# GpSimd without two-input elementwise work in a scheduled hybrid decoder layer

## The chip, the cores and the metric

The kernel runs on one core of a Trainium2 chip. A core has five engines with a queue each: TensorE (PE, with its weight loads PEld), VectorE (DVE), ScalarE (ACT), GpSimd (POOL) and SyncE (SP, which issues most transfers). The metric is the device time of one execution in microseconds (us); lower is better.

## The reference, cut to what matters

One layer on 512 tokens of width 1024, in float32. Three mixing groups read one normalized input and are merged by one output projection; then follows a SwiGLU feed-forward part.

```python
h = rmsnorm(x, norm_mix);  mem_h = rmsnorm(mem, norm_mem)
c_q, c_kv, k_rope, hq, hf, hi, hg, mq = split(h @ w_in)
# A) latent attention, 4 heads: q, k, v from low-rank c_q, c_kv; q, k normalized; the last 64
#    columns rotated by position (rope); causal softmax
a1, a2 = x[..., :32], x[..., 32:]
rope(x) = concat(a1 * cos - a2 * sin, a2 * cos + a1 * sin)
# B) gated linear recurrence (HGRN2), 4 heads, per head:
q = silu(hq) * 128 ** -0.5
f = lb + (1 - lb) * sigmoid(hf);  k = 1 - f
o[t] = sum over s <= t of (sum_d q[t,d] k[s,d] prod f[s+1..t, d]) v[s]
y_hg = rmsnorm(o) * silu(hg)
# C) cross-attention of 4 heads into 256 memory tokens, q and k normalized
x = x + concat(rmsnorm(y_mla), y_hg, rmsnorm(y_mem)) @ w_out
x = x + (silu(rmsnorm(x) @ w_gate) * (rmsnorm(x) @ w_up)) @ w_down
```

## The kernel before

Every float32 operand of a large matmul is split into two parts in a reduced format, hi and lo: `split` casts on ScalarE and subtracts on VectorE (L480). A product is then three matmuls, hi x hi, hi x lo, lo x hi (`mm3`, L510). Tiles are 128 partitions by up to 512 columns, with features on the partitions. The tags in the profile are the pools: `xh`, `xl` the split input, `wr` a raw weight piece, `wh`, `wl` its split, `hd`, `v`, `pth`, `ptl` split operands of attention, `td`, `tc`, `tm`, `y`, `mx`, `p` work tiles; `mm`, `at`, `tr` are the PSUM banks.

The body does not issue instructions. It records them, each with its home engine, and `Recorder.run` (L242) plays a list schedule: at each step it takes, over all engines, the operation that can start first by the prices in `price` (L187) and the latencies in `LAT`; ties go by priority. `first(0)` marks urgent work, `first(2)` work that fills gaps, such as weight projections. Some operations have alternatives on another engine (`others`, L160): casts and scalings of ScalarE may go to VectorE, and a VectorE product of two SBUF tiles may go to GpSimd with a handicap of 500 ns. `shares` (L222) marks operations of VectorE and GpSimd that exclude each other in the schedule. The engine queues then hold exactly the order found, so a change of a price or of an engine can move rows far from it. Nothing in the feed-forward part has the GpSimd alternative (`not self.base`), since `base` is set there (L1161).

The places that the change and the prediction touch:
- `hg_in` (L678): per head of group B the gate fg, its complement k_, and a clamp of fg.
- `hg_levels` (L738): scores by doubling block sizes m; at each level q and k_ are multiplied by prefix products (`tm<-tm,p`), q's half on VectorE, k_'s half on GpSimd.
- `hg_final` (L808): output gate z times its sigmoid (`td<-td,td`), then y times z, then the split of the result.
- `sumsq` (L548): squares on ScalarE, added up (`tc<-tc,tc`, `td<-td,td`), by default on GpSimd.
- `rope` (L939): two products with sin on GpSimd (`tc<-qr,n_t`), two with cos and two sums on VectorE (`qr<-qr,n`, `qr<-qr,tc`), each of which the scheduler may place on GpSimd. The sums for the memory group are in the same way on GpSimd (L851, L853).
- `fast` (L1229): one of three column chunks of the gate or the up projection, as seven products of half-size blocks: 1, 5 and 7 are copied out of PSUM, then 6, 2, 3 and 4 follow in that order and are added on VectorE. Sums of weight blocks are made by accumulating transfers on GpSimd's queue. After the up projection's product 4 the activations are formed on VectorE and transposed on TensorE (`tr<-cst,p`, `RX`, `qr`, `ptl`: the four column groups). In the first chunk there is no down projection yet to fill in.

Of the kernel before, what the change touches and what calls it, by code (L numbers as in the profile page):

```python
# [12 lines left out]
AF = mybir.ActivationFunctionType  # L13
ALU = mybir.AluOpType
AX = mybir.AxisListType

P = 128
# [28 lines left out]
class Recorder:  # L46
# [113 lines left out]
    def others(self, o, ins):  # L160

        a, k = o.args, o.kw
        sbuf = all(x.tensor.name not in self.tiles or self.tiles[x.tensor.name][4] == "SB" for x in ins)
        if o.eng == "scalar":
            if o.name == "copy":
                return [("vector", "tensor_copy", a, k)]
            if o.name == "activation" and a[2] == AF.Copy and set(k) == {"scale"}:
                return [("vector", "tensor_scalar", (a[0], a[1], k["scale"], None, ALU.mult), {})]
            if o.name == "activation" and a[2] == AF.Square and not k and sbuf:
                return [("vector", "tensor_tensor", (a[0], a[1], a[1], ALU.mult), {})]  # L170
        elif o.eng == "vector" and sbuf and not self.base:
            if o.name == "tensor_tensor" and len(ins) == 2 and a[3] != ALU.max and self._free(a[0]) >= 128 and a[0].ap[0][1] == 128:
                return [("gpsimd", "tensor_tensor", a, k)]
        elif o.eng == "gpsimd":
            if o.name == "tensor_tensor":
                return [("vector", "tensor_tensor", a, k)]
            if o.name == "tensor_scalar":
                return [("vector", "tensor_scalar", (a[0], a[1], a[2], None, ALU.mult), {}), ("scalar", "activation", (a[0], a[1], AF.Copy), {"scale": a[2]})]
            if o.name == "memset":
                return [("vector", "memset", a, k)]  # L180
        return []
# [5 lines left out]
    def price(self, o, outs, ins):  # L187
# [3 lines left out]
        if o.eng == "tensor":  # L191
            if o.name == "transpose":
                return 109
            if ins[0].dtype == F32R:
                return n / 2.4 + (15.5 if n >= 512 else 14) if n >= 256 else max(1.67 * n, 107)
            return 222 if n <= 2 else 64 if n <= 32 else 122 if n <= 64 else 226 if n <= 128 else 1.7 * n
        m = max([self._free(a) for a in ins] + [n])
# [205 lines left out]
def body(ctx, tc, t):  # L403
# [143 lines left out]

    def sumsq(srcs, acc=None, tag="td", eng=G):  # L548

# [128 lines left out]
    def hg_in(h):  # L678
        with rec.first(2):
# [7 lines left out]
            with rec.first(0):  # L687
                V.tensor_scalar(fg, s_, omlb[:, h:h + 1], lb[:, h:h + 1], ALU.mult, ALU.add)
                V.tensor_scalar(k_, fg, -1.0, 1.0, ALU.mult, ALU.add)
                V.tensor_scalar(fg, fg, 1.0, None, ALU.min)  # L690
# [47 lines left out]
    def hg_levels(q, k_, tot):  # L738
# [15 lines left out]
        while m <= 128:  # L754
# [29 lines left out]
            V.tensor_tensor(qv[:, :, 1, :], qv[:, :, 1, :], tv[:, :, 0:1].broadcast_to([P, n, m]), ALU.mult)  # L784
            G.tensor_tensor(kv[:, :, 0, :], kv[:, :, 0, :], tv[:, :, 1:2].broadcast_to([P, n, m]), ALU.mult)
            if m < 128:
# [21 lines left out]
    def hg_final(h, y):  # L808
        with rec.first(2):
            z, s_ = gated(13 + h)  # L810
        G.tensor_tensor(z, z, s_, ALU.mult)
        V.tensor_tensor(y, y, z, ALU.mult)
# [29 lines left out]
    with rec.first(1):  # L842
# [9 lines left out]
        ms2 = sb("td", (P, NM))  # L852
        G.tensor_tensor(ms2, ms[:, :NM], ms[:, NM:], ALU.add)  # L853
        rm = cp.tile([P, 2], F32, name="rm")
# [84 lines left out]
    def rope(src, nh):  # L939
# [4 lines left out]
        m = [sb("tc", (P, NB, nh, 32)) for i in range(2)]  # L944
        G.tensor_tensor(m[0], a1, bc(sin), ALU.mult)
        G.tensor_tensor(m[1], a2, bc(sin), ALU.mult)
        V.tensor_tensor(a1, a1, bc(cos), ALU.mult)
# [494 lines left out]
```

## Time and profile before

| | |
|---|---|
| median of 3 runs | 736.45 us (735.52 to 736.71) |
| profiled execution | 735.35 us |
| its span, first to last instruction | 733.3 us |
| mean granted TensorE clock | 0.998 |
| GpSimd products and sums of two tiles | 78, 75.0 us on GpSimd |
| other GpSimd work | 96 accumulating transfers, memsets, 4 scalings |

A row of a group reads: line, engine, operation, output<-inputs with their sizes, count, busy time in us and mean length in ns, then the idle time of the engine just before such instructions and what ended it. In a row by time, the first two numbers are start and length in us, and the idle time stands in brackets. All recorded instructions have one line (L378), so the tile names tell them apart. A name such as `n` in `qr<-qr,n` is the table of cosines, `n_t` that of sines.

### The profile page before, as it was taken

The page shows a single profiled execution, that of the slowest core. Times are in us where ns is not written, and L with a number is a line of the kernel's source. Part 1 is how long each engine was busy: PE and PEld are TensorE (multiplying, and loading weights), DVE is VectorE, ACT ScalarE, POOL GpSimd, SP SyncE. Part 2 cuts the span into 40 slices and gives each one's busy share as a digit, 9 for nine tenths or more (in the row PEclk, how much of TensorE's full clock was granted, in tenths as well). Part 3 has the DMA queues.
Part 4 walks back from the last instruction along what each step waited for, and adds up shares of the span by engine and source line. Part 5 has one row for each costly group of instructions (what it writes and reads, how often), then busy time and mean ns, then how long its engine had stood idle before and what let it go on. Part 6 is the DMA issues. An engine that isn't in the chain of part 4 may idle for free.

```text
span 733.3 us, 11253 instructions
## 1 busy us (share of the span) xinstructions
PE 717.2 (98%) x3788; PEld 608.1 (83%) x3788; DVE 557.7 (76%) x1257; ACT 371.8 (51%) x703; POOL 164.1 (22%) x202
## 2 busy tenths in 40 slices
PE   7999999999999999999999999899999999999997
PEld 6899888888788877788887888688888899999886
DVE  6987788875997799897899978938546777638742
ACT  6533324436764456566487564545553355643420
POOL 0133233214311112120123324212303213410000
PEclk9999999999999999999999999999999999999999
DMA  8230122102540232221899999969958767942242
GB/s 287 75 116 30 59 72 80 58 29 88 166 150 29 73 116 86 72 73 30 223 310 217 235 222 222 221 147 202 214 169 145 192 143 148 220 125 45 65 129 72
DMA packets 48009, 98.17 MB, mean 134 GB/s; under 512 B 5584, under 2 KB 15696, under 8 KB 47952
## 3 DMA queue, kind: packets, MB, share of 16 engines
q1 hardware_dynamic: 33696, 73.98, 31.2%
q0 software_dynamic: 13824, 23.07, 19.7%
q8 instruction: 30, 0.49, 0.3%
q10 hardware_dynamic: 432, 0.40, 0.2%
q14 instruction: 27, 0.22, 0.1%
HBM read 95.33 MB, written 2.10 MB: 133 GB/s over the span
## 4 chain that ended last, share of the span: by engine, by line
PE 91%; DVE 5%; ACT 3%; issue 1%; DMA 0%; DVEq 0%; ACTq 0%
PE mm L378 46%; PE at L378 24%; PE tr L378 21%; DVE wl L378 1%; DVE ptl L378 1%; ACT L378 1%; ACT wh L378 1%; DVE tm L378 1%; DMA tm<-in_xT 0%; ACT td L378 0%; ACT v L378 0%; DVE td L378 0%; DVE qr L378 0%; DVE hd L378 0%; DVE p L378 0%
## 5 line engine op out<-in xcount | busy, mean ns | idle before, releaser
L378 ACT CAST wh<-wr 128x512 fp32r<-128x512 f32 (+2 forms) x140 | 82.5, 597 | 113.3 <-PE mm L378 62.8
L378 DVE TENSOR_TENSOR wl<-wr,wh 128x512 fp32r<-128x512 f32 (+2 forms) x139 | 97.1, 704 | 31.9 <-issue 10.8
L378 PE MATMUL mm<-xh,wh 128*128 128x512 f32 x248 | 98.3, 401 | 4.4 <-ACT wh L378 3.6
L378 PE MATMUL mm<-xl,wh 128*128 128x512 f32 x248 | 99.5, 403 | 0.0
L378 PE MATMUL mm<-xh,wl 128*128 128x512 f32 x248 | 99.0, 401 | 0.0
L378 DVE TENSOR_TENSOR wl<-y,wh 128x512 fp32r<-128x512 f32 (+1 forms) x84 | 53.0, 637 | 44.1 <-PE tr L378 17.3
L378 ACT CAST wh<-y 128x512 fp32r<-128x512 f32 (+1 forms) x83 | 47.9, 582 | 63.5 <-PE at L378 33.2
L378 DVE TENSOR_TENSOR wl<-mx,wh 128x512 fp32r<-128x512 f32 (+1 forms) x72 | 45.9, 644 | 27.8 <-PE tr L378 17.2
L378 PE MATMUL mm<-wh,hd 128*128 128x512 f32 (+2 forms) x188 | 64.4, 369 | 0.7 <-ACT wh L378 0.7
L378 ACT CAST wh<-mx 128x512 fp32r<-128x512 f32 (+1 forms) x67 | 39.2, 585 | 43.8 <-PE at L378 25.6
L378 PEld LDWEIGHTS mm<-xh,wh 128*128 128x128 f32 x248 | 46.9, 190 | 13.2 <-ACT wh L378 3.8
L378 POOL DMA_DIRECT2D y<-in_wu x36 | 32.1, 948 | 96.9 <-DVE wl L378 69.9
L378 PEld LDWEIGHTS mm<-xl,wh 128*128 128x128 f32 x248 | 47.1, 190 | 8.0 <-DVE xl L378 0.4
L378 PEld LDWEIGHTS mm<-xh,wl 128*128 128x128 f32 x248 | 47.0, 190 | 8.0 <-DVE wl L378 0.4
L378 PE MATMUL at<-wh,hd 128*128 128x512 f32 (+1 forms) x132 | 49.6, 377 | 0.0
L378 PE MATMUL tr<-xl,wh 128*128 128x512 f32 x112 | 43.8, 391 | 0.0
L378 PE MATMUL tr<-xh,wl 128*128 128x512 f32 x112 | 43.7, 390 | 0.0
L378 PE MATMUL tr<-xh,wh 128*128 128x512 f32 x112 | 43.7, 390 | 0.0
L378 PEld LDWEIGHTS mm<-wh,hd 128*128 128x128 f32 x188 | 34.9, 190 | 6.3 <-ACT wh L378 1.4
L378 PEld LDWEIGHTS at<-tm,tm 128*128 128x128 f32 (+2 forms) x320 | 33.3, 170 | 7.4 <-issue 5.2
L378 PE MATMUL at<-tm,tm 128*128 128x128 f32 (+3 forms) x320 | 38.0, 263 | 0.9 <-DVE tm L378 0.8
L378 PE MATMUL mm<-wl,hd 128*128 128x512 f32 (+2 forms) x100 | 37.2, 372 | 0.0
(381 smaller groups left out, 1813.4 us busy)
## 6 DMA issues: line engine op xcount, KB each, us to landing
wr<-in_wf SPq DMA_DIRECT2D x19, 512.0 KB, 3.4
wr<-in_wd SPq DMA_DIRECT2D x16, 512.0 KB, 5.2
mx<-in_wg SPq DMA_DIRECT2D x24, 256.0 KB, 6.1
mx<-in_wu SPq DMA_DIRECT2D x24, 256.0 KB, 5.1
y<-in_wu POOLq DMA_DIRECT2D x24, 256.0 KB, 6.0
tm<-in_xT SPq DMA_DIRECT2D x16, 256.0 KB, 4.0
wr<-in_wt SPq DMA_DIRECT2D x8, 512.0 KB, 4.7
wr<-in_wo SPq DMA_DIRECT2D x8, 512.0 KB, 3.6
```

Source lines behind the costliest of these rows:

```text
L378: r = getattr(getattr(self.nc, o.eng), o.name)(*[get(a) for a in o.args], **{k: get(a) for k, a in o.kw.items()})
```

## The change

The GpSimd alternative for two-input work goes from `others`. The products and sums that had GpSimd as their home get VectorE: squares, rotations, the k_ half of the levels, the memory group's sum, the gate's product. Two affine steps of each gate head go from VectorE to ScalarE. Two prices change: a transpose from 109 to 109.5, a plain float32 matmul of 129 to 256 columns from 1.7 n (435.2 at 256) to 436. Memsets, some scalings and the accumulating transfers stay on GpSimd.

```diff
@@ others
-        elif o.eng == "vector" and sbuf and not self.base:
-            if o.name == "tensor_tensor" and len(ins) == 2 and a[3] != ALU.max and self._free(a[0]) >= 128 and a[0].ap[0][1] == 128:
-                return [("gpsimd", "tensor_tensor", a, k)]
@@ price
-                return 109
+                return 109.5
...
-            return 222 if n <= 2 else 64 if n <= 32 else 122 if n <= 64 else 226 if n <= 128 else 1.7 * n
+            return 222 if n <= 2 else 64 if n <= 32 else 122 if n <= 64 else 226 if n <= 128 else 436 if n <= 256 else 1.7 * n
@@ sumsq
-    def sumsq(srcs, acc=None, tag="td", eng=G):
+    def sumsq(srcs, acc=None, tag="td", eng=V):
@@ hg_in
-                V.tensor_scalar(fg, s_, omlb[:, h:h + 1], lb[:, h:h + 1], ALU.mult, ALU.add)
-                V.tensor_scalar(k_, fg, -1.0, 1.0, ALU.mult, ALU.add)
+                A.activation(fg, s_, AF.Identity, bias=lb[:, h:h + 1], scale=omlb[:, h:h + 1])
+                A.activation(k_, fg, AF.Identity, bias=ones[:, 0:1], scale=-1.0)
@@ hg_levels
-            G.tensor_tensor(kv[:, :, 0, :], kv[:, :, 0, :], tv[:, :, 1:2].broadcast_to([P, n, m]), ALU.mult)
+            V.tensor_tensor(kv[:, :, 0, :], kv[:, :, 0, :], tv[:, :, 1:2].broadcast_to([P, n, m]), ALU.mult)
@@ hg_final
-        G.tensor_tensor(z, z, s_, ALU.mult)
+        V.tensor_tensor(z, z, s_, ALU.mult)
@@ memory group
-        G.tensor_tensor(ms2, ms[:, :NM], ms[:, NM:], ALU.add)
+        V.tensor_tensor(ms2, ms[:, :NM], ms[:, NM:], ALU.add)
@@ rope
-        G.tensor_tensor(m[0], a1, bc(sin), ALU.mult)
-        G.tensor_tensor(m[1], a2, bc(sin), ALU.mult)
+        V.tensor_tensor(m[0], a1, bc(sin), ALU.mult)
+        V.tensor_tensor(m[1], a2, bc(sin), ALU.mult)
```

The first place is GpSimd's queue from the attention heads to the memory group (some 260 to 310 us of the profile before). `tc` are sums of squares, `hd` and `wl` splits, `td` the gate's product. Before:

```order
L378 TENSOR_TENSOR tc_4902<-tc_4902,tc_4667 128x512
L378 TENSOR_TENSOR tc_4914<-tc_4914,tc_4902 128x512
L378 MEMSET p_4982 128x128
L378 TENSOR_TENSOR hd_5030<-tm_4530,hd_5022 128x512
L378 TENSOR_TENSOR hd_5047<-tm_4649,hd_5037 128x512
L378 MEMSET p_5081 128x128
L378 TENSOR_TENSOR td_5112<-td_5112,td_5123 128x512
L378 TENSOR_TENSOR tc_5191<-tc_5191,tc_4914 128x512
```

The same part of GpSimd's queue now, up to its first accumulating transfer:

```order
L375 MEMSET p_5034 128x128
L375 MEMSET p_5115 128x128
L375 TENSOR_SCALAR p_5310<-p_5310,sm_5311 128x256
L375 TENSOR_SCALAR p_5643<-p_5643,sm_5644 128x256
L375 TENSOR_SCALAR p_5773<-p_5773,sm_5774 128x256
L375 DMA xl_5905<-in_wg 128x512
```

Only memsets and three scalings of softmax weights are left ahead of the transfers; the sums, splits and gate products have gone to VectorE's queue.

The second place is VectorE's queue at the same point of the program, around the gate product of a group B head (`td`) and the last sum of squares of group A (`tc_5191` before, `tc_5257` now). Before:

```order
L378 TENSOR_TENSOR xl_5140<-y_2621,xh_5128 128x512
L378 TENSOR_TENSOR wl_5148<-wr_4963,wh_5108 128x512
L378 TENSOR_TENSOR xl_5156<-y_2908,xh_5134 128x512
L378 TENSOR_TENSOR ptl_5164<-tr_5115,pth_5152 128x512
L378 TENSOR_TENSOR ptl_5164<-tr_5117,pth_5152 128x512
L378 TENSOR_TENSOR y_3208<-y_3208,td_5112 128x512
```

VectorE's queue there now:

```order
L375 TENSOR_TENSOR hd_5171<-tm_4459,hd_5107 128x512
L375 CAST xh_5178<-y_3288 128x512
L375 TENSOR_TENSOR td_5142<-td_5142,td_5154 128x512
L375 TENSOR_TENSOR xl_5188<-y_3288,xh_5178 128x512
L375 TENSOR_TENSOR y_3644<-y_3644,td_5142 128x512
L375 RECIPROCAL sm_5175<-sm_5175 128x1
L375 TENSOR_TENSOR hd_5196<-tm_4585,hd_5111 128x512
```

The gate product (`td_5142`) and the splits `hd` of the attention heads now stand between VectorE's own rows.

The third place is TensorE's queue at the end of the first feed-forward chunk. `tr<-cst,ptl` are the transposes of the last activation quarter; `mm` and `at` rows with `hd` are of the next chunk's gate product (left factor a weight, right factor the normalized input), those with `pth` of the up projection's product 4. Before:

```order
L378 MATMUL at_7026<-wh_7076,pth_6445 128x512
L378 MATMUL at_7026<-wl_7086,pth_6445 128x512
L378 MATMUL at_7026<-wh_7076,pth_6468 128x512
L378 MATMUL mm_7106<-wh_7101,hd_6092 128x512
L378 MATMUL at_7108<-wh_7101,hd_6092 128x512
L378 MATMUL mm_7111<-wh_7104,hd_6196 128x512
L378 MATMUL at_7113<-wh_7104,hd_6196 128x512
L378 MATMUL tr_7068<-cst,ptl_6874 128x128
```

TensorE's queue there now:

```order
L375 MATMUL at_7071<-wh_7042,pth_6471 128x512
L375 MATMUL mm_7109<-wh_7085,hd_6220 128x512
L375 MATMUL mm_7109<-wl_7102,hd_6220 128x512
L375 MATMUL mm_7109<-wh_7085,hd_6239 128x512
L375 MATMUL at_7118<-wh_7085,hd_6220 128x512
L375 MATMUL at_7118<-wl_7102,hd_6220 128x512
L375 MATMUL at_7118<-wh_7085,hd_6239 128x512
L375 MATMUL mm_7109<-wh_7111,hd_6220 128x512
L375 MATMUL at_7118<-wh_7111,hd_6220 128x512
L375 MATMUL mm_7129<-wh_7116,hd_6087 128x512
L375 MATMUL tr_7063<-cst,ptl_6883 128x128
```

Nine rows of the next gate product stand between product 4 and the transposes of `ptl`, where there were four.

## Prediction

> **What bounds the kernel now.** I read the page first, then the busy time by stretches, then the rows around TensorE's longest pauses. The page and the chain that ended last:
>
> ```profile
> span 733.3 us, 11253 instructions
> PE 717.2 (98%) x3788; PEld 608.1 (83%) x3788; DVE 557.7 (76%) x1257; ACT 371.8 (51%) x703; POOL 164.1 (22%) x202
> PE 91%; DVE 5%; ACT 3%; issue 1%; DMA 0%; DVEq 0%; ACTq 0%
> ```
>
> TensorE is busy for 98% of the span and owns 91% of the chain. The change leaves every matmul in place, so it can win or lose only TensorE's pauses (733.3 - 717.2 = 16.1 us), and stretches in which its clock is reduced. Where the pauses lie, by stretches (columns: length; then busy us of PE, PEld, DVE, ACT, POOL; granted clock; DMA):
>
> ```profile
> 40.00:160.00 120.00, 119.12 (x812) 104.27 (x811) 95.95 (x263) 43.62 (x86) 38.73 (x56) 1.00 0.18 59
> 160.00:260.00 100.00, 98.84 (x550) 82.88 (x548) 79.47 (x221) 58.88 (x122) 22.05 (x25) 1.00 0.30 98
> 260.00:420.00 160.00, 157.03 (x798) 129.09 (x799) 147.25 (x335) 101.82 (x202) 36.54 (x39) 1.00 0.56 154
> 360.00:380.00 20.00, 20.00 (x89) 16.24 (x88) 19.59 (x38) 14.29 (x28) 3.49 (x4) 1.00 1.09 296
> 400.00:420.00 20.00, 19.97 (x93) 16.24 (x92) 19.83 (x34) 12.33 (x22) 7.54 (x10) 1.00 0.97 229
> 460.00:480.00 20.00, 17.77 (x85) 13.95 (x84) 16.51 (x26) 12.25 (x22) 4.35 (x5) 0.91 0.92 207
> ```
>
> Between 40 and 260 TensorE pauses 0.9 + 1.2 us. It pauses 3.0 us from 260 to 420, where VectorE is 92% busy, and 2.2 us in the one stretch 460 to 480, the only one of these with a clock under 1.00. Two kinds of pause are in these numbers.
>
> **First kind: collisions.** Three times a GpSimd operation of the sort that is removed overlaps a VectorE operation with two SBUF inputs, and TensorE pauses right behind (time, length, engine, operation; in brackets the idle time and its releaser):
>
> ```profile
> 266.09 1.29 POOL L378 TENSOR_TENSOR tc<-tc,tc 128x512 f32<-128x512 f32 x1 [11.00 <-ACT tc L378]
> 266.50 1.42 DVE L378 TENSOR_TENSOR tc<-y 128x512 f32<-128x512 f32 x1 [0.31 <-PE tr L378]
> 268.80 0.48 PE L378 MATMUL at<-hd,hd 128*128 128x256 f32 x2 [0.80 <-DVE hd L378]
> ...
> 285.26 0.68 DVE L378 TENSOR_TENSOR wl<-wr,wh 128x512 fp32r<-128x512 f32 x1
> 287.44 1.41 POOL L378 TENSOR_TENSOR td<-td,td 128x512 f32<-128x512 f32 x1 [7.07 <-ACT td L378]
> 287.71 1.68 DVE L378 TENSOR_TENSOR wl<-wr,wh 128x512 fp32r<-128x512 f32 x1
> 290.65 0.39 PE L378 MATMUL at<-ptl,v 128*128 128x256 f32 x1 [0.64 <-DVE ptl L378]
> 293.38 1.29 POOL L378 TENSOR_TENSOR tc<-tc,tc 128x512 f32<-128x512 f32 x1 [4.54 <-ACT tc L378]
> 293.43 1.79 DVE L378 TENSOR_TENSOR wl<-wr,wh 128x512 fp32r<-128x512 f32 x1 [0.45 <-PE mm L378]
> 298.52 0.50 PE L378 MATMUL mm<-xh,wh 128*128 128x512 f32 x1 [0.80 <-DVE xh L378]
> ```
>
> The same split takes 0.68 us alone and 1.68 or 1.79 us beside GpSimd: VectorE loses 0.7, 1.0 and 1.1 us and TensorE then pauses 0.80, 0.64 and 0.80. A 512-wide product given to GpSimd thus cost VectorE as much as doing it.
>
> **Second kind: the end of the first feed-forward chunk.** The transposes of the last activation quarter (ptl) wait for a VectorE chain that runs unbroken from the first row here:
>
> ```profile
> 445.80 0.69 DVE L378 TENSOR_TENSOR qr<-mm,p 128x512 f32<-128x512 f32 x1 [0.61 <-PE mm L378]
> 453.62 1.89 DVE L378 TENSOR_TENSOR wl<-y,wh 128x512 fp32r<-128x512 f32 x3
> 462.39 1.41 DVE L378 SCALAR_TENSOR_TENSOR ptl<-ptl,r,tc 128x512 f32<-128x512 f32 x2
> 463.20 0.51 PE L378 MATMUL tr<-cst,ptl 128*128 128x128 f32 x2 [2.08 <-DVE ptl L378]
> 463.86 0.69 PE L378 MATMUL tr<-cst,ptl 128*128 128x128 f32 x2 [0.15 <-DVE ptl L378]
> 465.48 0.63 PE L378 MATMUL at<-wl,hd 128*128 128x512 f32 x1
> 465.91 0.63 PE L378 MATMUL at<-wh,hd 128*128 128x512 f32 x1
> 468.38 0.40 PE L378 MATMUL at<-wl,hd 128*128 128x512 f32 x1
> 468.62 0.39 PE L378 MATMUL at<-wh,hd 128*128 128x512 f32 x1
> ```
>
> After the 2.08 us pause matmuls start 0.43 us apart, later 0.24. The granted clock of 0.91 over 20 us is worth 1.8 us. The pauses of 0.8 us above left the clock at 1.00. So this event costs 2.2 + 1.8 = 4.0 us.
>
> **The change, part by part.** The groups that carry its price:
>
> ```profile
> L378 POOL TENSOR_TENSOR tm<-tm,p 128x256 f32<-128x256 f32 x32 | 22.3, 705 | 51.4 <-PE at L378 43.1 <-issue 4.9 <-DVE p L378 1.7
> L378 DVE TENSOR_TENSOR tm<-tm,p 128x256 f32<-128x256 f32 x24 | 10.4, 436 | 0.0
> L378 DVE TENSOR_TENSOR wl<-wr,wh 128x512 fp32r<-128x512 f32 x123 | 89.9, 737 | 25.3 <-issue 10.8 <-PE mm L378 6.4 <-PE at L378 3.0
> L378 DVE TENSOR_SCALAR tm<-td,omlb,lb 128x512 f32<-128x512 f32 x4 | 2.6, 644 | 0.0
> L378 ACT ACTIVATE tc<-tc,r 128x512 f32<-128x512 f32 x6 | 4.1, 716 | 0.0
> ...
> L378 POOL TENSOR_TENSOR hd<-tm,hd 128x512 fp32r<-128x512 f32 x3 | 3.9, 1288 | 12.6 <-ACT hd L378 7.0 <-DVE p L378 5.6
> L378 POOL TENSOR_TENSOR tc<-kr,n_t 128x128 f32<-128x128 f32 x1 | 0.9, 915 | 0.0
> ...
> L378 POOL TENSOR_TENSOR tc<-tc,tc 128x512 f32<-128x512 f32 x4 | 5.1, 1286 | 23.5 <-ACT tc L378 22.8 <-DVE tc L378 0.7
> L378 POOL TENSOR_TENSOR td<-td,td 128x512 f32<-128x512 f32 x1 | 1.4, 1410 | 7.1 <-ACT td L378 7.1
> ```
>
> 78 operations leave GpSimd: 45 of 256 elements, 30 of 512, 3 others. On VectorE one of 512 costs 0.60 (the three splits at 453.62: 1.89 less 0.69, halved), one of 256 costs 0.42: 45 x 0.42 + 30 x 0.60 + 1.1 = 38 us. Less the stretching that goes: in the split group alone 123 x (737 - 684) ns = 6.5 us. Less the eight affine steps, 2.6 + about 2.1 us. Some casts come back from ScalarE, some 2 us. VectorE should show 557.7 + 38 - 6.5 - 4.7 + 2 = 586 us, 580 to 590. GpSimd should show about 88 us.
>
> From 40 to 160 VectorE has 24 us of idle time for its share there (41 operations of 256 elements, 6 of 512: 21 us, less stretching and affine steps) and TensorE 119.12 of 120 from dense projections that fill in: nothing. If that cover were gone, the latency of a gate head would show: two ScalarE steps of 0.72 instead of two on VectorE of 0.64 and less; the clamp of fg on VectorE waits for ScalarE's second step, with weight splits queued behind it; at most some 0.5 us for each of four heads.
>
> From 160 to 420 lie 28 of the moved operations, 17 before 260 and 11 after (the last four rows are the first and last group of each). 24 of 512 and four smaller: 15.9 us. The stretched operations there give back 5.3 us (three shown give 2.8). Net 10.6 us into 260 - 79.47 - 147.25 = 33 us of idle. Lower end 0: the rows 360:380 and 400:420 have VectorE at 19.59 and 19.83 of 20 and TensorE at 20.00 and 19.97. Upper end 10.6. I take +1.5, near the lower end, since two rows at that load show it.
>
> The three collision pauses go: 0.80 + 0.64 + 0.80 = -2.2 (ends -2.2 and 0). What is late next there is the same VectorE queue.
>
> The order at the end of the first chunk changes most. From the last matmul of product 6 (whose result starts the VectorE chain at 445.80) to the first ptl transpose stand 69 TensorE rows before and 88 now, nine instead of four of them from the next gate product. VectorE's chain has three splits more in it, 3 x 0.60: 17.3 + 1.8 + 0.2 = 19.3 us until the transposes may start. TensorE's rows last 84 x 0.23 + 4 x 0.11 = 19.8 us from a start about 0.5 before. The pause should shrink from 2.2 to 0.3 or less, too short for the clock to fall, as the 0.8 us pauses show: -3.7 (ends -4.0 and 0). By the Trainium skill (TensorE: Matmul & The Clock Gate, Part 1) the clock halves only after an idle window of about 3.4 us; the 2.08 us pause is shorter and the rows behind it are slow all the same, so here the trace decides.
>
> The start (TensorE's first 120 rows) and everything from the second chunk's first gate product on stand in the same order: 0. Memory loads swap places in a dozen rows of SP's queue; GpSimd's accumulating loads wait for VectorE's splits today, not for the products ahead of them: 0. The altered prices only set the order.
>
> Sum: -2.2 - 3.7 + 1.5 = -4.4 us. The profiled execution took 735.35 (733.3 and 2.05 around it), 1.1 below the median of 736.45; 736.45 - 4.4 = 732.0.
>
> **Rivals.** (1) VectorE becomes the bound between 160 and 420, in strict order, with softmax reductions and weight splits behind the moved products. For it: 92% busy from 260 on. Against: the two rows at 98%. Every moved us that TensorE does not cover counts; it decides for slower when 7.4 of the 15.9 us land on TensorE (5.9 gained and 1.5 of margin); at two thirds, -5.9 + 10.6 = +4.7: 741.
> (2) The chunk's pause stays, because VectorE gets there later than counted; the margin is only half a us. Then -2.2 + 1.5: 735.7, no change.
> (3) The collision pauses come back as queueing: -3.7 + 1.5: 734.3.
> (4) The pause goes but the slow stretch comes anyway: -2.2 - 1.9 + 1.5: 733.9. The slow rows right behind the pause, and nowhere else in this chunk, speak against it. The rule of the Trainium skill (TensorE: Matmul & The Clock Gate, Part 1) speaks for it.
>
> **How the numbers follow.** Forecast 0.50, rivals 0.17, 0.15, 0.13, 0.05. A measurement here tells 0.2% (1.5 us) from no change. Faster: 0.50 + 0.13 + 0.05 = 0.68; same 0.15; slower 0.17. Low end: 4.0 instead of 3.7, no cost on VectorE, and 1.5 more from other pauses: -7.7, so 728. High end: part of rival 1, 738.5.
>
> **What would show it.** No stretched split over 0.8 us; no pause of 0.6 us between 265 and 300; clock 1.00 around 460 and less than 1 us of idle there; VectorE near 586. I am wrong if TensorE's pauses from 160 to 420 grow beyond 6 us or the slow stretch at the first chunk's end stays.

## The result, and the profile after

The changed kernel takes 743.74 us (median, 743.49 to 744.80) against 736.54 us for the kernel before on the same chip: a ratio of 1.0099, 95% interval 1.0085 to 1.0113. It is slower by 7.2 us where 4.4 us of gain were forecast, and the time lies outside the range.

The head of the page after, the chain that ended last, and the group of the weight splits:

```profile
span 742.9 us, 11191 instructions
PE 726.4 (98%) x3788; PEld 613.5 (83%) x3788; DVE 573.0 (77%) x1321; ACT 381.5 (51%) x717; POOL 90.9 (12%) x124
PE 91%; DVE 6%; ACT 2%; issue 1%; DMA 0%; DVEq 0%; ACTq 0%
L375 DVE TENSOR_TENSOR wl<-wr,wh 128x512 fp32r<-128x512 f32 (+2 forms) x148 | 96.4, 656 | 28.4 <-issue 10.9
```

GpSimd shows 90.9 us (88 forecast) and VectorE 573.0 (586 forecast, 580 to 590). TensorE's own busy time grew by 9.2 us with the same 3788 matmuls, while its pauses grew by only 0.4 (16.1 to 16.5), so most of the loss shows as matmuls that took longer, and not as waiting. The stretches of after (columns as in the prediction: length; busy us of PE, PEld, DVE, ACT, POOL; granted clock; DMA):

```profile
40.00:160.00 120.00, 119.58 (x800) 103.70 (x799) 101.19 (x284) 47.41 (x92) 1.80 (x9) 1.00 0.20 63
160.00:260.00 100.00, 99.22 (x545) 83.85 (x544) 81.83 (x227) 56.88 (x117) 1.61 (x6) 0.97 0.30 92
260.00:420.00 160.00, 153.53 (x760) 123.98 (x759) 143.18 (x351) 100.20 (x203) 18.55 (x24) 0.97 0.51 134
160.00:180.00 20.00, 19.32 (x119) 17.86 (x118) 12.27 (x51) 5.91 (x14) 0.20 (x1) 0.83 0.19 54
300.00:320.00 20.00, 16.16 (x69) 12.58 (x68) 14.90 (x38) 6.91 (x14) 0.48 (x1) 0.74 0.14 39
360.00:380.00 20.00, 18.50 (x88) 14.38 (x87) 16.69 (x36) 9.57 (x17) 4.08 (x5) 1.00 0.92 251
460.00:480.00 20.00, 19.84 (x95) 16.08 (x94) 20.00 (x34) 9.29 (x17) 7.86 (x9) 1.00 1.04 238
```

Two of the same stretches before, which the prediction did not show:

```profile
160.00:180.00 20.00, 19.77 (x124) 17.25 (x123) 10.66 (x33) 10.67 (x23) 5.55 (x6) 1.00 0.26 80
300.00:320.00 20.00, 20.00 (x110) 16.80 (x110) 18.41 (x47) 14.59 (x32) 4.75 (x4) 1.00 0.25 76
```

To put one number on a stretch I take its **excess**: over TensorE's instructions there, the distance from one start to the next, less the step that the same shape shows at full clock (0.227 us for 512 columns, 0.12 for 256, 0.11 for 128 and for 2, and so on). It counts pauses and slow clock alike. Over the whole execution it is 29.9 us before and 39.5 after (other steps shift both alike: 31.5 and 41.1 with the median step of each shape), and the difference of 9.6 is that of the spans (742.9 - 733.3; the profiled execution of before was a short one of its kind and that of after a long one, so the medians differ by less, 7.2).

| stretch | excess before | after | forecast of the change | measured |
|---|---|---|---|---|
| 0 to 40 | 6.7 | 7.6 | 0 | +0.9 |
| 40 to 160 | 6.4 | 6.4 | 0 | -0.1 |
| 160 to 260 | 3.8 | 6.8 | +1.5, with 300 to 420 | +3.1 |
| 260 to 300 (collisions) | 3.6 | 2.0 | -2.2 | -1.6 |
| 300 to 420 | 3.3 | 14.1 | see above | +10.8 |
| 420 to 460 | 0.1 | 0.3 | 0 | +0.2 |
| 460 to 480 (end of the first chunk) | 4.4 | 0.6 | -3.7 | -3.8 |

So three places carry the loss: 160 to 180 (+3.9), 300 to 320 (+8.7) and 360 to 380 (+2.3).

**The place at 305.** It is the normalization of the latent attention's outputs. Rows of TensorE and VectorE after (start, length, engine, operation; in brackets the idle time and its releaser):

```profile
304.63 0.42 DVE L375 COPY y<-at 128x256 f32<-128x256 f32 x1 [1.18 <-PE at L375]
305.09 0.69 DVE L375 TENSOR_TENSOR tc<-y 128x512 f32<-128x512 f32 x1
305.13 0.40 PE L375 MATMUL mm<-xh,wl 128*128 128x512 f32 x1
305.70 0.68 DVE L375 TENSOR_TENSOR wl<-wr,wh 128x512 fp32r<-128x512 f32 x1
306.30 0.68 DVE L375 TENSOR_TENSOR tc<-tc,tc 128x512 f32<-128x512 f32 x1
307.13 1.02 PE L375 MATMUL tr<-ones,tc 128*128 128x2 f32 x8 [1.60 <-DVE tc L375]
308.99 0.54 PE L375 MATMUL at<-hd,hd 128*128 128x256 f32 x2 [0.56 <-ACT hd L375]
310.19 1.22 PE L375 MATMUL at<-hd,hd 128*128 128x256 f32 x4 [0.65 <-DVE hd L375]
313.76 2.08 PE L375 MATMUL mm<-mx,wh 128*128 128x512 f32 x4 [0.85 <-ACT mx L375]
```

The last output of attention is copied, squared, summed, column-summed on TensorE (tr<-ones,tc), and only then can the normalized mx be made, 6.6 us later. TensorE has little other work left: four pauses of 3.7 us together, and the clock falls (0.74 over 20 us). Before, the same column sum stood here:

```profile
295.50 0.95 PE L378 MATMUL tr<-ones,tc 128*128 128x2 f32 x8
296.31 0.49 PE L378 MATMUL mm<-xl,wh 128*128 128x512 f32 x1
305.44 0.65 PE L378 MATMUL mm<-mx,wh 128*128 128x512 f32 x2
```

It waited for nothing, and the 9.9 us to the first mx matmul were filled, among others, by 26 matmuls of the output projection's HGRN half (xh, xl). In the changed kernel's order exactly these 26 (26 x 0.227 = 5.9 us) stand ahead of the column sum. They were spent earlier.

**The place at 168.** Rows of TensorE after:

```profile
167.98 1.05 PE L375 MATMUL tr<-ones,tc 128*128 128x2 f32 x8 [0.16 <-ACT tc L375]
168.89 1.48 PE L375 MATMUL tr<-ones,td 128*128 128x2 f32 x12
171.35 0.62 PE L375 MATMUL tr<-cst,sm 128*128 128x128 f32 x4 [0.51 <-DVE sq_n L375]
171.81 0.95 PE L375 MATMUL tr<-ones,td 128*128 128x2 f32 x8
172.89 3.58 PE L375 MATMUL tr<-ones,td 128*128 128x2 f32 x16
176.33 0.56 PE L375 MATMUL mm<-wl,hd 128*128 128x256 f32 x1
176.69 0.63 PE L375 MATMUL mm<-wh,hd 128*128 128x256 f32 x2
```

Six groups of two-column matmuls (column sums of squares: 44 of them in 8 us) stand together, where before they were spread over the projections of the query heads. The only pauses are 0.16 and 0.51 us, yet from 172.8, when 28 of the 44 have run, each step takes twice as long (16 in 3.58 us; 8 took 0.95 just ahead).

**What came as forecast.** No stretched split is left, the three pauses at 266 to 299 are gone, and the end of the first chunk runs at clock 1.00 with 0.16 us of pause. The transposes of ptl there no longer wait:

```profile
475.44 0.38 PE L375 MATMUL tr<-cst,ptl 128*128 128x128 f32 x2
```

### The profile page after: what moved, and what is told of

It reads as the page before. It is cut to its first block, busy times and chain, and to the rows that moved or that the text cites. A ratio compares the mean times of both kernels' runs of the same rounds, so it can differ in the third digit from the quotient of the medians.

```text
span 742.9 us, 11191 instructions
## 1 busy us (share of the span) xinstructions
PE 726.4 (98%) x3788; PEld 613.5 (83%) x3788; DVE 573.0 (77%) x1321; ACT 381.5 (51%) x717; POOL 90.9 (12%) x124
## 4 chain that ended last, share of the span: by engine, by line
PE 91%; DVE 6%; ACT 2%; issue 1%; DMA 0%; DVEq 0%; ACTq 0%
PE mm L375 46%; PE at L375 23%; PE tr L375 22%; DVE wl L375 1%; DVE sm L375 1%; DVE ptl L375 1%; ACT L375 1%; DVE y L375 1%; DMA tm<-in_xT 0%; DVE td L375 0%; DVE hd L375 0%; DVE tc L375 0%; DVE qr L375 0%; DVE xl L375 0%; DVE tm L375 0%
## 5 line engine op out<-in xcount | busy, mean ns | idle before, releaser
L375 ACT CAST wh<-wr 128x512 fp32r<-128x512 f32 (+2 forms) x133 | 79.3, 598 | 118.0 <-PE mm L375 72.4
```

Of the source, the lines that this page charges most:

```text
L375: r = getattr(getattr(self.nc, o.eng), o.name)(*[get(a) for a in o.args], **{k: get(a) for k, a in o.kw.items()})
```

## The experiments

Theory A at the start: the new order of the rows costs the time, and the work moved to VectorE does not. Theory B: the moved work costs it, whatever the order. Four kernels separate assignment, order, prices and the affine steps. First, the order of before on every engine, row for row, with only the engine of the 78 products changed when they are issued:

```diff
     order = rec.run()
+    for o_ in order:
+        if o_.eng == "gpsimd" and o_.name == "tensor_tensor":
+            o_.eng = "vector"
```

> Every queue keeps the order of the kernel before, row for row; only the 78 two-input operations that stood on GpSimd are issued on VectorE at the same place in the program. The affine steps stay on VectorE. Theory A (the new order costs the time, the load on VectorE does not): 732 to 737, with the collision pauses between 265 and 300 gone and the 2.1 us pause at the first chunk's end still there. Theory B (VectorE's added load costs it, whatever the order): 740 or more, with TensorE's pauses from 160 to 420 beyond 6 us.

Measured: 744.07 us, ratio 1.0098 (1.0074 to 1.0122). By the time B holds and A falls: in the old order the moved work alone costs 7.8 us. But B's place was wrong: TensorE's pauses from 160 to 420 are 4.6 us, not beyond 6. The loss is many small pauses, two thirds of it from 40 to 160, where I had priced nothing (excess there 12.2 against 6.4). The collision pauses are gone and the pause at the first chunk's end is still there (2.10 us), as A had it. The stretch, and one of its pauses:

```profile
40.00:160.00 120.00, 116.69 (x779) 98.56 (x779) 102.60 (x284) 41.13 (x83) 1.93 (x10) 1.00 0.19 60
53.93 0.68 DVE L378 TENSOR_TENSOR wl<-wr,wh 128x512 fp32r<-128x512 f32 x1
54.53 0.48 DVE L378 SCALAR_TENSOR_TENSOR v<-tr,rx,v 128x256 fp32r<-128x256 f32 x1
55.16 0.36 PE L378 MATMUL tr<-wh,xh 128*128 128x256 f32 x1 [0.87 <-DVE v L378]
```

A weight split that GpSimd used to do stands in VectorE's queue ahead of the step that reads v out of PSUM, and TensorE waits 0.87 us for it.

Second, the reverse: the changed kernel's order, with some 60 products that had GpSimd as their home issued there again (GpSimd then shows 150.0 us). They are recorded for VectorE, so that the plan is that of the changed kernel, and marked:

```diff
+        back = eng == "gpsimd" and name == "tensor_tensor"
+        if back:
+            eng = "vector"
...
     order = rec.run()
+    for o_ in order:
+        if o_.back:
+            o_.eng = "gpsimd"
```

> Every queue keeps the order of the changed kernel; the operations whose home was GpSimd before (level products, squares' sums, sin products, gate products) are issued on GpSimd again at the same place, some 50 of the 78; the freely placed ones stay on VectorE. Theory A: 741 to 748, with the long pause before group A's norm still there and collisions back. Theory B: 738 or less, since VectorE is relieved of some 25 us.

Measured: 750.16 us, ratio 1.0179 (1.0153 to 1.0206). This is above A's range and far from B's. A's signs are there: a pause of 2.03 us ahead of the norm's column sum, and stretched VectorE operations again. The new order is bad with most of the old assignment too, and the three places are there again (excess 5.7 at 160, 9.4 at 300, 3.8 at 360). So neither theory explains both kernels. The four corners are 736.2 (old order, GpSimd), 744.1 (old order, VectorE), 750.2 (new, 60 of the 78 on GpSimd), 743.7 (new, VectorE): the moved work costs in the old order, which was planned without it, and the new order has something of its own that costs. The corners are not quite clean: the affine steps go with the order, and 18 of the 78 products stay on VectorE in the third.

Third and fourth, two small parts of the change: the altered prices taken back, and only the affine steps moved.

```diff
-                return 109.5
+                return 109
...
-            return ... else 436 if n <= 256 else 1.7 * n
+            return ... else 1.7 * n
```

> The changed kernel with the two prices of the kernel before; all operations on the same engines but the order of some rows. Theory A: the time moves by more than 1.5 us either way if the rows around group A's norm and the run of column sums change, and stays at 743 to 745 if both are as in the changed kernel. Theory B: within 1.5 us of 743.7, since the load is the same.

Measured: 744.77 us, ratio 1.0111 (1.0085 to 1.0137), the same three places, which fits both theories. The prices make no difference that these runs can tell.

```diff
-                V.tensor_scalar(fg, s_, omlb[:, h:h + 1], lb[:, h:h + 1], ALU.mult, ALU.add)
-                V.tensor_scalar(k_, fg, -1.0, 1.0, ALU.mult, ALU.add)
+                A.activation(fg, s_, AF.Identity, bias=lb[:, h:h + 1], scale=omlb[:, h:h + 1])
+                A.activation(k_, fg, AF.Identity, bias=ones[:, 0:1], scale=-1.0)
```

> The kernel before with one part of the change: the two affine steps of each gate head on ScalarE. GpSimd keeps its work. Both theories: 735 to 738; the steps lie from 30 to 120 us, where TensorE is covered by projections. Over 738.5 would mean that this part has a price of its own.

Measured: 738.31 us, ratio 1.0025 (1.0012 to 1.0037): a small loss, 2.1 us, with one new pause of 1.0 us at 102.4. It lies just above the range and under the 738.5 that I had named for a price of its own. A part at most, and not the 7 us.

**Where in the old order the moved work costs.** The first kernel again, with only the first 49 products (up to 150 us) moved.

```diff
+    moved = [o_ for o_ in order if o_.eng == "gpsimd" and o_.name == "tensor_tensor"]
+    for o_ in moved[:49]:
+        o_.eng = "vector"
```

> The kernel before with its order frozen row for row, and only the first 49 of GpSimd's 78 tensor operations (up to 150 us) issued on VectorE at the same places; the other 29 stay on GpSimd. All 78 gave 744.07 us against 736.22. My prediction priced this stretch at nothing. Theory A (by the excess of TensorE's steps in that kernel's trace: 5.8 us more from 40 to 160, 3.1 more from 160 to 340): 741 to 743. Rival B (the stretch is covered by projections, and the loss comes from the 29 late ones): 736 to 738.

Measured: 740.81 us, ratio 1.0051 (1.0036 to 1.0067): 4.4 us, just under A's range and far from B's; the other 29 then make some 3.5 (7.85 - 4.36, not run by themselves). The row 40 to 160 is that of the kernel with all 78 moved (TensorE 116.72 of 120).

**A sharper theory for the new order.** My theory is that the plan hides VectorE's longer queue by pulling filler matmuls forward, so that 40 to 160 looks untouched (119.58 of 120). But the filler is a fixed stock. The attention heads come later and later against TensorE's other work: counted in matmul time ahead of them, the first head's scores stand 2.3 us later than before, the second's 3.6, the third's 5.9, the fourth's 7.3, the norm's column sum 5.9. At the norm the stock is gone. If so, VectorE's load as such is harmless, and a plan that ranks attention first must give the time back with every product still on VectorE.

> The changed kernel with the attention heads ranked first in the plan (class 0 in place of 1), nothing else; no operation goes back to GpSimd. In this plan the norm's column sum after attention stands 3.1 us of matmul work earlier than before the change, and 9 us earlier than in the changed kernel. Theory A (order: late attention used up the reserve of w_out matmuls): the excess of 9.1 us from 300 to 320 falls below 2 us and the clock there stays at 1.00; the time is 733 to 738. Rival B (VectorE is simply too full from 160 to 300): the pauses move to where the steps behind attention are now late, and the time stays at 741 or above.

```diff
     ym = []
-    for h in range(4):
-        ...                      # attention heads, group_norm unchanged
+    with rec.first(0):
+        for h in range(4):
+            ...
```

Measured: 736.82 us, ratio 1.0001 (0.9991 to 1.0011). A holds: the time is that of the kernel before.

```profile
160.00:180.00 20.00, 19.32 (x112) 18.14 (x111) 11.70 (x49) 5.69 (x13) 0.20 (x1) 0.75 0.17 54
300.00:320.00 20.00, 20.00 (x109) 16.60 (x108) 18.86 (x49) 15.16 (x33) 1.12 (x2) 1.00 0.26 79
294.10 0.95 PE L375 MATMUL tr<-ones,tc 128*128 128x2 f32 x8
```

The column sum stands at 294.10 without a wait, the excess from 300 to 320 is 0.4 in place of 9.1, and VectorE is fuller there than in the changed kernel (18.86 of 20 against 14.90). The heads themselves do not stand earlier throughout: the first one's scores stand 5.9 us later than before the change, the fourth's 2.7; it is the norm's column sum that stands 3.2 earlier, and with it the stock that is left. Two of the three places stay: 168 is still slow, and the pause of 1.25 us that was at 370 is now at 360. The gains at 266 to 299 and at the first chunk's end make up for them.

Put back by half, the same dose works by half. The home engines of the old kernel, without VectorE's freedom to hand its own steps to GpSimd:

```diff
-    def sumsq(srcs, acc=None, tag="td", eng=V):
+    def sumsq(srcs, acc=None, tag="td", eng=G):
...
-        V.tensor_tensor(z, z, s_, ALU.mult)
+        G.tensor_tensor(z, z, s_, ALU.mult)
...
```

> The changed kernel with only the home engines put back (squares' sums, key products of the levels, gate products and rotations are GpSimd's by home again, about 40 tensor operations run there), while VectorE's own steps still may not go to GpSimd; planned anew. Theory A (VectorE's longer queue makes the attention heads late against TensorE's order, the reserve of w_out matmuls is used up to cover that, and the bill comes at the norm after attention, 305 to 320): in this plan the norm's column sum stands 3.7 us of matmul work later than before (5.9 in the changed kernel), so the loss there shrinks but stays: 738 to 742. Rival B (the loss is VectorE's plain load, whatever the order): half of the work is back, so half of the loss, 739 to 741, spread over all stretches. Rival C (any new plan is bad where GpSimd and VectorE collide): 745 or more.

Measured: 737.70 us, ratio 1.0011 (0.9998 to 1.0023), a little under A's range. The loss at 300 shrank with the column sum's lateness (3.7 us of excess at 3.7 us of lateness, 9.1 at 5.9, 0.4 before), while the place at 168 ran at clock 1.00. The first chunk's end is slow again (4.5 us of excess).

The control for it: the kernel before with attention ranked first.

> A control: the kernel before, its work on GpSimd as it was, with the attention heads ranked first in the plan. Theory A (ranking repairs the lateness that the change brought; the kernel before had an excess of 0.39 us from 300 to 320 and nothing to gain there): 734.5 to 738, with the excess from 300 to 320 still below 1 us. Rival B (ranking attention first is a gain of its own, and says nothing of the change): 733 or less.

Measured: 741.44 us, ratio 1.0069 (1.0057 to 1.0082). It is no gain of its own; it is a loss there, 4.7 us, more than A allowed (excess from 160 to 220 of 5.2 us against 2.6, and 2.0 at 300). The rank suits the new assignment only.

**The clock at 168.** Three groups of column sums are set apart in the changed kernel's order, everything else frozen:

```diff
+    for ns, n in (((1404, 1405, 1406, 1407), 1471), ((1408,), 1474), ...):
+        later(ns, n)             # move these rows to stand ahead of row n
```

> The changed kernel with its order frozen, but for three groups of four two-column matmuls (column sums of td) and their copies, which stand 9 to 27 rows later on TensorE, between the projections that followed them; same work, same assignment. Theory A (a dense run of two-column matmuls, 10 groups in 8 us, lets the granted clock fall, with no long pause): the clock from 160 to 180 is 1.00 in place of 0.83, the excess there falls from 4.5 us to below 1.5, and the time is 3 to 4 us less than the changed kernel's: 739.5 to 741. Rival B (the clock fell for the pauses of 0.16 and 0.51 us at 168 and 171): those stay, the clock stays at 0.83, 743 to 744.

Measured: 741.76 us, ratio 1.0071 (1.0047 to 1.0095), 2.0 below the changed kernel and just above A's range. In the profiled execution (741.64) A's mechanism holds: the two pauses are the same, the clock stays, and the excess from 160 to 180 is 1.3. One of the four executions (744.39, mean clock 0.987) is as slow as the changed kernel, so the clock was not safe here either.

```profile
160.00:180.00 20.00, 19.32 (x136) 17.51 (x135) 14.72 (x58) 8.94 (x20) 0.20 (x1) 1.00 0.19 55
167.90 1.05 PE L375 MATMUL tr<-ones,tc 128*128 128x2 f32 x8 [0.16 <-ACT tc L375]
171.27 0.62 PE L375 MATMUL tr<-cst,sm 128*128 128x128 f32 x4 [0.52 <-DVE sq_n L375]
172.44 0.95 PE L375 MATMUL tr<-ones,td 128*128 128x2 f32 x8
177.07 0.95 PE L375 MATMUL tr<-ones,td 128*128 128x2 f32 x8
```

Both repairs together should then have added:

> The changed kernel with both repairs: attention heads ranked first in the plan, and the three groups of two-column matmuls spread. The first alone gave 736.82 us, the second alone 741.76, the changed kernel 743.74. Theory A (the loss is those two places of the new order): they add, since they lie 130 us apart; of the 5.97 us of excess that the first still has from 160 to 180, all but about 1.3 go: 732 to 734, faster than before the change (736.4), with the clock at 1.00 from 160 to 180. Rival B (a place in front merely shifts the wait behind): 736 or more.

Measured: 736.92 us, ratio 0.9995 (0.9978 to 1.0013). A fell, and the median lies in B's range, though not by B's reason: of 12 executions four took 733.1 to 733.6 at a mean granted clock of 1.000, as A had it, and eight took 736.8 to 738.7 at 0.990 to 0.992. In the profiled one the clock fell at 170, ahead of the groups that I had moved:

```profile
170.01 1.09 PE L375 MATMUL tr<-cst,sm 128*128 128x128 f32 x4 [0.52 <-DVE sq_n L375]
172.17 1.70 PE L375 MATMUL tr<-ones,td 128*128 128x2 f32 x8
```

The case is marginal: the same program keeps the clock or loses it. The Trainium skill (TensorE: Matmul & The Clock Gate, Part 1) has the clock follow TensorE's activity in windows of about 3.4 us that run free of the kernel. The traces here agree: every half-speed stretch between 25 us and the last few matmuls lasts one, two or three times 3.41 us, and the changed kernel's two falls, at 172.79 and 309.33, lie 136.54 us apart, 40 times 3.41. Cut along these borders, the stretches at the fall in the changed kernel, then at the end of the first chunk in the kernel before, then at the same point in the kernel with the old order and all 78 products on VectorE (its borders are reckoned back from the only fall in its trace, at its end):

```profile
169.38:172.79 3.41, 2.90 (x25) 2.72 (x25) 3.18 (x24) 1.20 (x2) 0.00 (x0) 1.00 0.00 0
172.79:176.20 3.41, 3.41 (x17) 3.31 (x16) 0.95 (x6) 0.38 (x1) 0.00 (x0) 0.50 0.00 0
460.02:463.43 3.41, 1.33 (x7) 0.77 (x5) 3.41 (x6) 0.00 (x0) 0.86 (x1) 1.00 1.10 295
463.43:466.84 3.41, 3.26 (x10) 2.09 (x9) 3.41 (x7) 2.11 (x4) 1.76 (x2) 0.50 0.78 130
468.73:472.15 3.42, 1.86 (x9) 1.19 (x7) 3.42 (x7) 0.00 (x0) 0.97 (x2) 1.00 1.10 298
472.15:475.56 3.41, 2.48 (x13) 1.67 (x14) 3.41 (x6) 1.84 (x4) 1.36 (x2) 1.00 0.78 158
```

Before the change the pause of 2.08 us lies in one window, and the next window runs at half speed. In the other kernel a pause of 2.10 us lies across a border, 1.55 us on one side, and the clock stays. I sorted the windows of all 17 traces, from 25 us on, by what TensorE did in them. With fewer than five two-column matmuls in a window, 1.94 us or more of pauses was followed by half speed each time (9 windows), and 1.66 us or less never. With 13 to 20 of them, pauses of 0.24 to 0.69 us were enough (8 windows), and 0.23 us or less were not; with 10 of them 0.52 us was not. Four windows with 5 to 8 of them and 1.61 us of pauses or more make up the rest of the falls. So pauses and two-column matmuls count together, inside one window. In the execution above, the window ahead of the fall holds 20 two-column matmuls and 0.56 us of pauses. That the four fast executions of this program had the borders elsewhere is likely, but none of them was profiled.

Setting all groups apart by hand brought two new pauses instead (0.69 at 169.6 and 0.47 at 176.3), and the mean clock was 0.988 to 0.993 in nine of 11 executions. A fell; B does not follow either, since the pauses are new. (The expectation says 7 of 12 for the kernel above; counted again, it is 8.)

```diff
+    later((1459, 1460, 1461), 1388)
+    later((1462, 1463, 1464, 1465, 1466, 1467, 1471, 1472, 1473), 1123)
```

> The changed kernel with attention ranked first and all five groups of two-column matmuls set apart, the first two groups as well (six matmuls of the projections stand between the third group and the transposes, and three between the second and the third). With only the last three groups apart, 7 of 12 runs lost the clock at 170 us (736.8 to 738.7 us) and the others kept it (733.1 to 733.6). Theory A (the share of short matmuls over a few microseconds decides, and that share was marginal at 166 to 170): the clock is 1.00 from 160 to 180 in nearly every run, the excess there is below 1.5 us, and the median is 732.5 to 734, faster than before the change (736.6). Rival B (the fall comes by chance, whatever stands there): again about half of the runs at 737, median 735 to 737.

Measured: 737.47 us, ratio 1.0006 (0.9990 to 1.0022).

So I let the plan place the sums: each ranked first, so that it stands where its squares are ready. Two kernels, with and without attention ranked first, in which the memory norm's sum was ranked first too:

```diff
             sq = sumsq([o])
-        V.tensor_copy(sq_n[:, :, h], colsum(sq, NB))
+            V.tensor_copy(sq_n[:, :, h], colsum(sq, NB))      # inside rec.first(0)
...
-        V.tensor_scalar(vm, colsum(ms2, 2), 1.0 / D, EPS, ALU.mult, ALU.add)
+        with rec.first(0):
+            V.tensor_scalar(vm, colsum(ms2, 2), 1.0 / D, EPS, ALU.mult, ALU.add)
```

> The changed kernel with attention ranked first and, in the plan, the column sums of the query heads and of the memory's norm ranked first too (class 0), so that each group of two-column matmuls stands where its squares are ready, between 512-wide projections, and no longer in one run behind them. Theory A (the crowd of two-column matmuls and the 256-wide ones around it starve TensorE's clock at 166 to 180): the clock there is 1.00 in every run and the excess below 1.5 us; 731.5 to 734, faster than the kernel before (736.6). Rival B (clock falls by chance): median 736 to 738.

> The changed kernel with only those column sums ranked first in the plan; attention stays as in the changed kernel. In this plan the norm's column sum after attention stands 2.8 us of matmul work later than before, against 5.9 in the changed kernel and 3.7 in the one with the home engines put back, which had an excess of 3.7 us from 300 to 320. Theory A (two places, two causes): the place at 160 to 180 is repaired (3.3 us) and the place at 300 to 320 keeps 2 to 5 us: 735 to 739. Rival B (the loss is VectorE's load and moves): 741 or more.

Measured: 740.27 us (1.0043, 1.0027 to 1.0059) with attention first, 744.08 (1.0093, 1.0075 to 1.0110) without. By time A fell in both; 744.08 lies in the range of the second one's B. By place, the second did as A said: excess 0.9 at clock 1.00 from 160 to 180, 3.0 from 300 to 320 (but 4.2 from 360 to 380); what spoils both is new, 120 to 140, 5 to 6 us more than in the changed kernel. Rows of the first:

```profile
120.00:140.00 20.00, 16.14 (x104) 13.76 (x102) 17.69 (x64) 7.56 (x16) 0.61 (x3) 0.83 0.10 35
122.84 0.73 DVE L375 SCALAR_TENSOR_TENSOR hd<-mm,smv,hd 128x512 fp32r<-128x512 f32 x1
123.50 0.74 DVE L375 TENSOR_TENSOR tm<-tm,p 128x256 f32<-128x256 f32 x2
124.39 0.68 PE L375 MATMUL at<-tm,tm 128*128 128x128 f32 x4 [2.02 <-DVE tm L375]
```

VectorE now takes a step of another path (hd) ahead of the gate levels' step (tm) that TensorE waits for. TensorE pauses 2.02 us, and the clock falls behind that pause. In the first of the two the clock at 160 to 180 was 0.91, so even this order was not safe there. A wait for VectorE that moves elsewhere is what the second one's B named; ranking work first has a price of its own. Without the memory norm's sum:

> The changed kernel with attention ranked first and the column sums of the query heads ranked first, but the memory norm's sum where it was: in the kernel where that one was ranked first too, its chain stood in front of the gate levels' steps and TensorE waited 6 us more from 120 to 132. Here TensorE's order up to 155 us is word for word that of the kernel with attention ranked first alone, and from there each group of two-column matmuls stands between 512- or 256-wide ones. Theory A (the crowd of short matmuls takes the clock at 166 to 180): clock 1.00 there in nearly every run, the excess from 160 to 180 below 1.5 us in place of 5.97, that from 120 to 140 at about 1.5 as in the changed kernel, and the median 732 to 734, faster than the kernel before (736.6). Rival B (chance): half of the runs at 737 or more, median 735 to 738.

Measured: 735.02 us, ratio 0.9977 (0.9966 to 0.9988). The median lies 1 us above A's range, at the low end of B's, but no execution reaches the 737 us that B expects of half of them. In the profiled execution (733.61) the place is as A said:

```profile
160.00:180.00 20.00, 19.50 (x133) 17.56 (x132) 14.74 (x52) 9.46 (x21) 0.28 (x1) 1.00 0.17 54
300.00:320.00 20.00, 20.00 (x110) 16.51 (x109) 18.95 (x46) 14.52 (x35) 1.41 (x2) 1.00 0.29 92
```

This is the one version faster than both kernels, by 0.23% against the kernel before. All its products are on VectorE, as in the changed kernel; only two ranks in the plan differ. Of its 12 executions three kept a mean clock of 1.000 (733.4 to 733.8) and nine lie at 0.995 to 0.997 (734.6 to 735.8). Only one of the first sort was profiled, so where the others lose the clock, at this place or another, is open.

**One repair that did not carry over.** The place at 360 to 380 is the memory attention's norm. Ranking its heads first too, on top of attention first and three sums apart:

> The changed kernel with both repairs and the four heads of the memory attention ranked first too; in this plan the second norm's column sum stands 10.6 us of matmul work earlier. Theory A (a norm whose column sum comes when the reserve of w_out matmuls is used up leaves TensorE waiting): the pause of 1.5 us at 358 goes, 0.5 to 2 us less than the kernel with both repairs alone. Rival B (that pause is not from the order, or the wait returns elsewhere before 380): the same time within 0.5 us.

Measured: 742.13 us, ratio 1.0060 (1.0034 to 1.0087). A fell, and the time is 5 us above B's too. The pause at 358 is gone (excess 0.4 from 340 to 360 against 1.9), but in the profiled execution, one of its short ones (738.14), the wait came back around it, as the second half of B has it: 2.1 at 300, 1.7 at 360, 2.2 at 420 and 4.4 at 460. So the third of the three places, 2.3 us, has no experiment that explains it.

## Why the prediction was wrong

- **Collisions, -2.2:** right, -1.6. The stretched operations and the three pauses are gone.
- **End of the first chunk, -3.7:** right, -3.8; the count of rows against VectorE's chain held, and the clock stayed at 1.00.
- **GpSimd 88, VectorE 586:** 90.9 and 573.0. VectorE came out 13 us lower than the sum, so the load was overestimated and the time underestimated: load was not the measure.
- **"From 160 to 420 ... I take +1.5":** this term failed. It measured +13.9 (3.1 + 10.8), above even its upper end of 10.6. I set VectorE's extra microseconds against its idle time in a fixed order, and took the end near zero because VectorE ran at 98% in two rows without harm. What counts was where each dependent step stands against TensorE's order. I had the order of both kernels and compared it at the first chunk, where it paid; I did not count how many w_out matmuls were left behind the norm's column sum (26 fewer), which would have shown the bill, and the kernel with attention ranked first shows that this was it for the place at 305 (excess 9.1 to 0.4 us), the largest part. The +3.1 from 160 to 260 is the fall of the clock at 168, for which the sum had no term; what caused the 2.3 us at 360 to 380 stays open.
- **"From 40 to 160 ... nothing":** the row came out as forecast (119.58 of 120), but the reason did not hold. In the unchanged order the first 49 products cost 4.4 us. That the plan paid for them out of filler that was needed at 305 fits the 26 matmuls, but was not shown by itself. The 0.5 us per gate head of the affine steps were taken as covered; alone, replanned, they cost 2.1 us.
- **"The pauses of 0.8 us left the clock at 1.00 ... too short for the clock to fall":** failed as a rule. At 168 to 173 the clock fell after pauses of 0.16 and 0.51 us among 28 two-column matmuls; at 305 to 320 it fell over several pauses of 0.6 to 1.6 us. What decides is the sum over one window of 3.41 us, and not the length of one pause. At 305 to 320 the price came to over double the pauses: 3.7 us of pause made 8.7 of excess.
- **"I am wrong if TensorE's pauses from 160 to 420 grow beyond 6 us":** they are 0.8 + 6.5 = 7.2 us. **Rival 1** had the sign and nearly the size (741), but not the mechanism: VectorE is less busy there than before (143.18 of 160 against 147.25 from 260 on, though the slowed stretch also holds less of the program: 760 matmul rows against 798), and with attention ranked first it takes the same work at no loss. Rival 1's mechanism, weight splits in VectorE's strict order ahead of what TensorE waits for, is what the kernel with the old order shows, mostly before 160.

On the rule weighed in the prediction (the Trainium skill, TensorE: Matmul & The Clock Gate, Part 1: an idle window of about 3.4 us): a 2.02 us pause, with one of 0.71 behind it, was again followed by a clock of 0.83 over 20 us, and 0.51 us of pauses among 15 two-column matmuls, in one window, by 0.83 in the changed kernel. A window need not be idle throughout for the clock to fall, and idle time alone does not set it here; the measurement decides.

## What to carry to other kernels

Where a planner reorders the work, a stretch that looks untouched may have been paid for with filler; count, at each place where TensorE must wait for a chain of small steps, how much independent matmul work stands behind it before and after. Move work to a busier engine together with the ranks in the plan: the same assignment gave 743.7, 736.8 and 735.0 us under three rankings, and the same ranking cost the old assignment 4.7. Do not let many short matmuls and a pause stand within the same few microseconds: here 13 to 20 two-column matmuls with 0.24 us of pauses or more in 3.41 us were followed by half speed.

## What the hardware did that I had not expected

- The clock is granted in windows of 3.41 us, and the same pause costs or not by where the borders lie: 2.08 us inside one window was followed by half speed for 3.41 us, 2.10 us across a border was not.
- Two-column matmuls help to take the clock without a long pause: 15 in one window with a pause of 0.51 us, then 0.22 us each in place of 0.11, and half speed for 6.8 us. Three groups moved apart, with the pauses unchanged, left 10 in the window, and the clock stayed at 1.00 in the profiled execution. Up to 19 in a window without a pause left it at 1.00 as well.
- The fall is a matter of a margin: one program took 733.1 to 733.6 us in 4 executions and 736.8 to 738.7 in 8, told apart by the mean granted clock alone (1.000 against 0.990 to 0.992). Differences below some 4 us between orders of this kernel need enough executions to see both.
